# Hidden units of a squared-ReLU MLP kept in DRAM as two parts, one more pair by seven products, and waits of TensorE moved (a two-layer hybrid decoder trunk, fp32)

## The chip, the cores and the metric

The kernel runs on one core of one Trainium2 chip. The metric is the device time of one execution in microseconds; lower is better. Three executions of the kernel before took 2156.13, 2157.28 and 2156.48 us, so the median is 2156.48. A profile was taken of one more execution, of 2157.01 us.

## The reference

Two layers over 256 tokens of width 2048, all in float32. With P the combined projection (1024 columns each of q, k, v, gate_b, gate_c, conv_in):

```python
for l in range(2):
    h = rmsnorm(x, attn_norm_g[l])
    q, k, v, gate_b, gate_c, conv_in = split(h @ w_in[l])        # w_in: 2048 x 6144
    A = diff_attention(qk_norm(q), qk_norm(k), v, lam, rel_bias)  # 8 heads, two maps each
    A = rmsnorm(A, subln_g[l]) * (1 - lam_init)
    C = gate_b * short_conv3(gate_c * conv_in)
    x = x + concat([A, C]) @ w_out[l]                             # 2048 x 2048
    hm = rmsnorm(x, mlp_norm_g[l]) @ w_up[l]                      # 2048 x 8192
    x = x + square(relu(hm)) @ w_down[l]                          # 8192 x 2048
```

The weights are read once per execution; most of the work is the matrix products with them.

## The kernel before

**Products in two parts.** A float32 value is kept as a high part in the type fp32r (a copy by ScalarE, which rounds) and a low part (value minus high part, a subtraction by VectorE). A product is the sum of three matmuls, high by high, high by low, low by high: `TERMS` (line 42). Each weight tile is loaded by a DMA from SyncE's queue, split by ScalarE and VectorE into `hi` and `lo` (class `Weights`, lines 287 to 371) and used by TensorE. `Weights.take` (line 357) hands out the next tile and has the next three (`AHEAD`) made ahead of it.

**The order of the work.** TensorE executes its instructions in the order in which the program issues them. The other engines' instructions are put in an order by a scheduler when the kernel is built, except those that are pinned to program order by `late` (line 122). Small pieces of work that need TensorE (transposes for the norms, attention) are generators kept by `Background` (line 59). After every few matmuls the program calls `work.tick()`, and a piece goes on when its count of ticks has run out; `work.start(piece, wait)` sets the first count. So the number of ticks says where in TensorE's order a transpose lands.

**The mixer** (line 711) runs for two halves of four heads the projections q, k and v and starts `attention` (line 579) behind each as a background piece; the conv path follows, then the output projection `o`. After each 512-column chunk of x is updated, `Norm.chunk` (line 443) is started: it transposes the chunk by TensorE into PSUM banks (`tpn`, from a pool of three), splits the transposed values into the parts `nT` (lines 270 and 271), and sums the squares (`squares`, line 463, on ScalarE).

**The MLP** (line 785) walks the 8192 hidden columns as 32 pairs of 256 (`NP`). In the up stage (line 986 on), pair i gets its two columns by `up_part` (32 matmuls of 128x512 and 32 of 128x256), `evict` adds the two PSUM halves into `h`, and `square` applies ReLU, the ratio of the norms and the square. Two pairs later (`LAG`), the left half of the down projection (output columns 0 to 1023) is formed with pair i's units by the seven products of a Strassen-like scheme (Winograd's form): a 2x2 block product by seven products of blocks (`product`, line 979) in place of eight. It needs sums of blocks of the weights (`quarters`, line 823, with VectorE) and of the units (`S1` to `S4`). Each pair by seven products is 21 matmuls of 128x512; by the ordinary way it is 24 (`ordinary`, line 1052). The last two pairs of the left half are done the ordinary way; before them `seven_onto` (line 1039) adds the seven products to x.

The units are also needed for the right half (columns 1024 to 2047), which comes after the whole up stage. They are therefore written to DRAM from GpSimd's queue: `hid`, one tile per block of four 128-unit groups, 256 KB for an ordinary pair (lines 961 and 962), and `hid7`, 512 KB with the block sums, for the eight pairs of `SEVEN` (line 39), which the right half forms by seven products. In the right half `pair(i)` (line 1083) reads units back into `back`, and ScalarE and VectorE split them into `fb` (lines 1079 and 1080), one pair ahead of TensorE in program order and up to four buffers deep (`apool`). Pairs 24 to 29 are read as blocks 12 to 14 and done column chunk by column chunk (`columns`, line 1105); chunk 2 of the output is one step ahead of chunk 3 (`order`, line 890). At the end of each chunk two instructions `onto` (line 1035) add the accumulators to x, and either the next layer's `norm.chunk` is started or the result is stored.

For the first pair of the up stage, both columns go into one PSUM tile of two banks (line 991), and column 0 is evicted before column 1's last matmuls are issued (lines 996 and 997). The first two forms of its weight tile (`plain`, the splits of single quarters, and `sums`, the block sums and their splits) are made by `forms["begin"]`, called after the square (line 999).

## Time and profile before

| | before |
|---|---|
| median of three executions | 2156.48 us |
| profiled execution | 2157.01 us |
| its span, from the first to the last instruction | 2155.2 us |
| mean granted TensorE clock | 0.999 |
| TensorE busy | 2136.4 us (99%) |
| VectorE busy | 1696.0 us (79%) |
| ScalarE busy | 1335.9 us (62%) |
| GpSimd busy | 160.3 us (7%) |
| DMA traffic | 452.91 MB, mean 210 GB/s |
| of it from GpSimd's queue | 44.17 MB |

One execution was recorded by the hardware profiler, and times in it are counted from the start of the span. In the view of the groups, "out<-in" gives the program's names for the tiles, then partitions x elements and type, and "mean" is the time of one instruction from its start to its end. Matmuls overlap each other, so their mean is longer than the distance from one start to the next. In the view of the waits, "PE pr L1059 <- DVE f L974: 3.0, 2, 1.5" reads: TensorE's instructions of line 1059 on the tile pr waited for VectorE's instruction of line 974 on f, 3.0 us in all, in 2 places, the longest 1.5 us. In the timeline each line is a start, a duration, engine and line, the operation, a count where several of one kind stand together, and in brackets the idle time ahead of it and what ended it. PE is TensorE, PEld its weight load, DVE VectorE, ACT ScalarE, POOL GpSimd, SP SyncE. The work of layer 1 follows that of layer 0 at a distance of about 1073 us: the same wait is found at 164 and at 1237 us.

### The profile page before, as it was taken

How to read it: one execution, taken by the hardware profiler on the slowest of the kernel's cores; microseconds unless marked ns; L12 is line 12 of the kernel's file. 1: busy time of each engine (PE TensorE's matmuls, PEld its weight loads, DVE VectorE, ACT ScalarE, POOL GpSimd, SP SyncE). 2: the span in 40 equal slices, each digit the busy share in tenths (PEclk: the TensorE clock that was granted, in tenths of full speed). 3: DMA queues.
4: the chain of work that ended last, by engine and by line, in shares of the span. 5: the costliest groups of instructions: out<-in, count | busy, mean ns of one | idle time of the engine just before them, and what ended most of it. 6: DMA issues, size and time to landing. Idle time of an engine off the chain costs nothing. (4 is left out here: it accounts for less than half of the span.)

```text
span 2155.2 us, 29063 instructions
## 1 busy us (share of the span) xinstructions
PE 2136.4 (99%) x10940; PEld 1821.8 (85%) x10940; DVE 1696.0 (79%) x2315; ACT 1335.9 (62%) x1799; POOL 160.3 (7%) x228
## 2 busy tenths in 40 slices
PE   9999999999999999999999999999999999999999
PEld 8888888888888888888788888888888888888887
DVE  6777655699889898798666776557998889887985
ACT  6666445567666666566556664445767666675663
POOL 3111100000000000200001111000000000002000
PEclk9999999999999999999999999999999999999999
DMA  8555766577767667686555567655776676766863
GB/s 272 179 160 186 236 187 189 163 237 225 234 214 225 215 220 224 212 296 220 190 166 177 165 203 218 186 175 186 236 232 220 213 227 220 223 209 232 300 225 110
DMA packets 282044, 452.91 MB, mean 210 GB/s; under 512 B 10707, under 2 KB 191525, under 8 KB 281904
## 3 DMA queue, kind: packets, MB, share of 16 engines
q1 hardware_dynamic: 268768, 406.88, 59.6%
q0 software_dynamic: 13088, 44.17, 5.7%
q8 instruction: 85, 1.39, 0.3%
q14 instruction: 55, 0.45, 0.1%
q10 hardware_dynamic: 48, 0.02, 0.0%
HBM read 428.98 MB, written 22.04 MB: 209 GB/s over the span
## 5 line engine op out<-in xcount | busy, mean ns | idle before, releaser
L303 DVE TENSOR_TENSOR wlo<-raw,whi 128x1024 fp32r<-128x1024 f32 x286 | 354.1, 1240 | 237.4 <-ACT whi L302 232.7
L302 ACT ACTIVATE whi<-raw 128x1024 fp32r<-128x1024 f32 x286 | 302.9, 1060 | 321.6 <-PE o L386 73.6
L939 PE MATMUL upc<-nT,uhi 128*128 128x512 f32 x1920 | 477.7, 391 | 0.3 <-ACT ev L949 0.3
L811 ACT ACTIVATE uhi<-uraw 128x1024 fp32r<-128x1024 f32 x256 | 270.2, 1056 | 265.1 <-PE upc L939 235.8
L939 PEld LDWEIGHTS upc<-nT,uhi 128*128 128x128 f32 x1920 | 352.7, 188 | 68.9 <-ACT ev L949 0.7
L812 DVE TENSOR_TENSOR ulo<-uraw,uhi 128x1024 fp32r<-128x1024 f32 x256 | 312.2, 1220 | 83.2 <-ACT uhi L811 78.7
L939 PEld LDWEIGHTS upc<-nT,ulo 128*128 128x128 f32 x1920 | 261.9, 190 | 18.7
L939 PE MATMUL upc<-nT,ulo 128*128 128x256 f32 x1920 | 267.7, 282 | 0.0
L1059 PE MATMUL dn<-whi,fb 128*128 128x512 f32 x512 | 160.3, 389 | 0.0
L386 PE MATMUL o<-whi,cat 128*128 128x512 f32 x512 | 159.5, 390 | 0.0
L302 ACT ACTIVATE whi<-uraw 128x1024 fp32r<-128x1024 f32 x64 | 67.9, 1061 | 78.2 <-PE dn L1059 68.6
L1059 PEld LDWEIGHTS dn<-whi,fb 128*128 128x128 f32 x512 | 96.1, 188 | 20.1
L386 PEld LDWEIGHTS o<-whi,cat 128*128 128x128 f32 x512 | 96.2, 188 | 19.7
L386 PE MATMUL o<-wlo,cat 128*128 128x512 f32 x256 | 99.6, 389 | 0.0
L1059 PE MATMUL dn<-wlo,fb 128*128 128x512 f32 x256 | 99.6, 389 | 0.0
L303 DVE TENSOR_TENSOR wlo<-uraw,whi 128x1024 fp32r<-128x1024 f32 x64 | 78.2, 1221 | 23.4 <-ACT whi L302 23.4
L832 DVE TENSOR_TENSOR t24l<-t,t24h 128x1024 fp32r<-128x1024 f32 x76 | 92.9, 1223 | 3.8 <-ACT t24h L831 1.4
L832 DVE TENSOR_TENSOR t13l<-t,t13h 128x1024 fp32r<-128x1024 f32 x76 | 92.8, 1221 | 3.5 <-ACT t13h L831 2.1
L982 PE MATMUL pr<-t13h,f 128*128 128x512 f32 x240 | 93.8, 391 | 0.0
L832 DVE TENSOR_TENSOR b2l<-draw,b2h 128x1024 fp32r<-128x1024 f32 x76 | 92.4, 1216 | 0.8 <-ACT b2h L831 0.8
L845 DVE TENSOR_TENSOR t<-draw 128x1024 f32<-128x1024 f32 x76 | 92.5, 1217 | 0.0
L831 ACT ACTIVATE t24h<-t 128x1024 fp32r<-128x1024 f32 x76 | 79.9, 1051 | 8.3 <-PE dn L982 3.6
(403 smaller groups left out, 4147.8 us busy)
## 6 DMA issues: line engine op xcount, KB each, us to landing
uraw<-in_w_up_dram SPq DMA_DIRECT2D x128, 1024.0 KB, 6.1
raw<-in_w_in_dram SPq DMA_DIRECT2D x191, 512.0 KB, 4.0
draw<-in_w_down_dram SPq DMA_DIRECT2D x80, 1024.0 KB, 6.9
raw<-in_w_out_dram SPq DMA_DIRECT2D x64, 512.0 KB, 3.7
uraw<-in_w_down_dram SPq DMA_DIRECT2D x32, 1024.0 KB, 6.6
raw<-in_w_down_dram SPq DMA_DIRECT2D x16, 1024.0 KB, 5.0
hid<-h POOLq DMA_DIRECT2D x44, 256.0 KB, 3.7
back<-hid POOLq DMA_DIRECT2D x32, 256.0 KB, 4.2
```

Source lines behind the costliest of these rows:

```text
L302: pair = (nc.scalar.activation(hi, raw, AF.Copy), nc.vector.tensor_sub(lo, raw, hi.bitcast(F32)))
L303: nc.vector.tensor_sub(lo, raw, hi.bitcast(F32)))
L386: nc.tensor.matmul(acc[:, t], a.ap[:, pa, k % KG, t * P:(t + 1) * P], (hi, lo)[pw][:, j], start=(k == 0 and n == 0), stop=(k == nk - 1 and ...
L811: nc.scalar.activation(hi, src, AF.Copy)
L812: nc.vector.tensor_sub(lo, src, hi.bitcast(F32))
L831: keep(nc.scalar.activation(hi, src, AF.Copy))
L832: keep(nc.vector.tensor_sub(lo, src, hi.bitcast(F32)))
L845: keep(nc.vector.tensor_sub(t[:, 0:2], raw[:, :, 1], raw[:, 0]))
L939: nc.tensor.matmul(acc[:, 0] if part else acc, wt[:, k], a.ap[:, 0, k % KG] if part else a.ap[:, :, k % KG], start=(part == 0 and kh == 0 ...
L982: nc.tensor.matmul(prods[n], f[:, pa, a], b[pw], start=(start and m == 0), stop=(stop and m == 2))
L1059: nc.tensor.matmul(prods[p], f[:, pa, 2 * k + t], b[pw][:, n], start=(p in starts and k == 0 and m == 0), stop=(stop and k == 1 and m == 2))
```

## The change

1. `SEVEN` has nine pairs, (2, 4, 7, 9, 12, 14, 17, 19, 22), in place of eight.
2. For an ordinary pair, `hid` holds the two parts of the units, high and low, 512 KB of type fp32r, one tile per pair. They are written from `f` after its split instead of from `h` ahead of it. Reading them back is one DMA (for a block of two pairs, two) into `fb`, and neither ScalarE nor VectorE works on them. Pairs of `SEVEN` are kept, read and split as before.
3. Up stage, first pair: both columns are evicted after all their matmuls; `plain` is called ahead of the evictions and `sums` after the square. The split of the second pair's first weight tile is pinned to program order.
4. `seven_onto` takes no engine; its four adds are on VectorE in both halves, and for the left half they are issued after the two ordinary pairs instead of ahead of them.
5. `Norm.chunk`: the squares are summed at once, ahead of the transposes, except in the first norm of layer 0. At the end of a layer the chunks 0 and 1 of the next norm start after 6 and 11 ticks, not 8 and 16.
6. Attention of the second half of the heads starts after 9 ticks, not 6.
7. In the last layer the last block of chunk 3 is done token tile by token tile (`by_token`): all its matmuls for the first 128 tokens, then those for the other 128.

```diff
-SEVEN = (2, 5, 8, 11, 14, 17, 20, 23)
+SEVEN = (2, 4, 7, 9, 12, 14, 17, 19, 22)
...
             a = self.tiles[n].open()
+            at_once = (self.which, self.l) != (0, 0)
+            if at_once:
+                self.squares(n)
...
             self.tiles[n].ready = True
-            if (self.which, self.l) == (0, 0) and n < D // CH - 1:
+            if at_once:
+                return
+            if n < D // CH - 1:
                 yield 12 - 2 * n
             self.squares(n)
...
                 work.start(attention(l, qT, kT, kL, v, h0, cat[half], bias, tmp,
-                                     1 + half), 3 * (1 + half))
+                                     1 + half), 3 + 6 * half)
...
-                    nc.scalar.activation(hi, src, AF.Copy)
-                    nc.vector.tensor_sub(lo, src, hi.bitcast(F32))
+                    pair = (nc.scalar.activation(hi, src, AF.Copy),
+                            nc.vector.tensor_sub(lo, src, hi.bitcast(F32)))
+                    if (i, c, kh) == (1, 0, 0):
+                        for ins in pair:
+                            late(ins)
...
-                    begin = lambda: made.update(p=plain(), s=sums())
-                    forms["begin"] = begin
+                    forms["plain"] = lambda: made.update(p=plain())
+                    forms["sums"] = lambda: made.update(s=sums())
...
-            hid = [dram.tile([P, KG * S], F32, name=f"hid{l}{b}") for b in range(NB2 - 1)]
+            hid = {i: dram.tile([P, 2, 4 * P], F32R, name=f"hid{l}p{i}")
+                   for i in range(NP - LAG) if i not in SEVEN}
...
                 nc.scalar.activation(u, u, AF.Square)
-                if i not in SEVEN and i < NP - LAG:
-                    nc.gpsimd.dma_start(hid[i // 2][:, i % 2 * 2 * S:(i % 2 + 1) * 2 * S], u)
...
                 nc.vector.tensor_sub(f[:, 1, :n], h[:, :n], f[:, 0, :n].bitcast(F32))
+                if i in hid:
+                    nc.gpsimd.dma_start(hid[i], f[:, :, 0:4].rearrange("p a k c -> p a (k c)"))
                 return f
...
                             up_part(two[c], kh)
-                            if kh:
-                                evict(two[c], h[:, 2 * c:2 * c + 2])
+                    forms["plain"]()
+                    for c in range(2):
+                        evict(two[c], h[:, 2 * c:2 * c + 2])
                     fs[0] = square(0, h)
-                    forms["begin"]()
+                    forms["sums"]()
...
-                for dst, v in ((x11, e1), (x12, e4), (x21, e3), (x22, e3)):
-                    engine.tensor_tensor(dst, dst, v, op=ALU.add)
+
+                def add():
+                    for dst, v in ((x11, e1), (x12, e4), (x21, e3), (x22, e3)):
+                        nc.vector.tensor_add(dst, dst, v)
+
+                return add
...
-            seven_onto(0, nc.gpsimd)
+            add = seven_onto(0)
...
                 ordinary(fs[j], (8,) if j == NP - LAG else (), j == NP - 1)
+            add()
...
-            def read_back(src, pool, tag, n):
...
+            def pair(i, f=None, at=0):
+
+                if f is None:
+                    f = apool.tile([P, 2, 8, P], F32R, tag="a", name="fb")
+                if i not in SEVEN:
+                    nc.gpsimd.dma_start(
+                        f[:, :, at:at + 4].rearrange("p a k c -> p a (k c)"), hid[i])
+                    return f
+                back = fpool.tile([P, 8, P], F32, tag="h", name="back", bufs=1)
+                nc.gpsimd.dma_start(back.rearrange("p a c -> p (a c)"), hid7[i])
+                nc.scalar.activation(f[:, 0], back, AF.Copy)
+                nc.vector.tensor_sub(f[:, 1], back, f[:, 0].bitcast(F32))
+                return f
+
+            def block(b):
+
+                pool, tag = (fpool, "f") if b == BLK else (apool, "a")
                 f = pool.tile([P, 2, 8, P], F32R, tag=tag, name="fb")
+                for j in range(2):
+                    pair(2 * b + j, f, 4 * j)
                 return f
...
+            def by_token(f, n):
+
+                parts = [weights.take() for _ in range(KG // 2)]
+                for t in range(NT):
+                    for k in range(KG):
+                        for m, (pa, pw) in enumerate(TERMS):
+                            nc.tensor.matmul(
+                                accs[n][:, t], f(k, pa, t), parts[k // 2][pw][:, k % 2],
+                                start=False, stop=(k == KG - 1 and m == 2))
+                        work.tick()
...
-            seven_onto(2, nc.vector)
+            seven_onto(2)()
             if not last:
-                work.start(norm.chunk(0, 2), 8)
-                work.start(norm.chunk(1, 2), 16)
+                work.start(norm.chunk(0, 2), 6)
+                work.start(norm.chunk(1, 2), 11)
...
-                columns(lambda k, pa, t, f=blocks[b]: f[:, pa, 2 * k + t], n,
-                        stop=(b == NB2 - 2))
+                units = lambda k, pa, t, f=blocks[b]: f[:, pa, 2 * k + t]
+                if last and (b, n) == order[-1]:
+                    by_token(units, n)
+                else:
+                    columns(units, n, stop=(b == NB2 - 2))
```

More of the change, by code (lines that the diff above doesn't have):

```diff
@@ L1037, in onto, with seven_onto @@
                                                op0=ALU.mult, op1=ALU.add)
-            def seven_onto(n, engine):
+            def seven_onto(n):
                 x11, x21, x12, x22 = (xs[n + i][:, t] for i in range(2) for t in range(NT))
@@ L1071, in mlp @@
                     onto(xs[n][:, t], prods[((2, 4), (3, 8))[n][t]], xs[n][:, t])
-            def read_back(src, pool, tag, n):
-                back = (fpool.tile([P, 8, P], F32, tag="h", name="back", bufs=1) if n == 8 else
-                        nat.tile([P, 4, P], F32, tag="wide", name="back"))
-                nc.gpsimd.dma_start(back.rearrange("p a c -> p (a c)"), src)
+            def pair(i, f=None, at=0):
[12 more added lines that the diff above has]
+                pool, tag = (fpool, "f") if b == BLK else (apool, "a")
                 f = pool.tile([P, 2, 8, P], F32R, tag=tag, name="fb")
-                nc.scalar.activation(f[:, 0, :n], back, AF.Copy)
-                nc.vector.tensor_sub(f[:, 1, :n], back, f[:, 0, :n].bitcast(F32))
-                return f
-            def pair(i):
-                if i in SEVEN:
-                    return read_back(hid7[i], apool, "a", 8)
-                return read_back(hid[i // 2][:, i % 2 * 2 * S:(i % 2 + 1) * 2 * S], apool, "a", 4)
-            def block(b):
-                return read_back(hid[b], *((fpool, "f") if b == BLK else (apool, "a")), 8)
+                for j in range(2):
+                    pair(2 * b + j, f, 4 * j)
+                return f
             def store(n):
```

## The prediction

> **What bounds the kernel now.** The page gives TensorE 2136.4 of 2155.2 us, so I first asked at what pace it issues and where it stands still. The matmul groups' mean of 390 ns is a latency. The pace stands in the windows and the timeline: ninety 128x512 matmuls fill 20 us, and two together last 0.62 where one lasts 0.39, so they start 0.227 apart.
>
> ```profile
> 1980.00:2000.00 20.00, 20.00 (x90) 16.54 (x89) 19.31 (x22) 13.47 (x16) 1.92 (x4) 1.00 1.01 360
> 2000.00:2020.00 20.00, 20.00 (x90) 16.57 (x89) 19.94 (x22) 12.42 (x15) 2.15 (x4) 1.00 0.88 316
> 1069.19 0.62 PE L1112 MATMUL dn<-whi,fb 128*128 128x512 f32 x2
> ```
>
> (The windows' columns: TensorE, its weight loads, VectorE, ScalarE, GpSimd, granted clock, DMA share, GB/s.) The time is therefore the number of matmuls times the pace, plus what TensorE waits. VectorE at 19.94 of 20 us here costs nothing, since all ninety matmuls ran. TensorE's waits, second view:
>
> ```profile
> PE pr L1059 <- DVE f L974: 3.0, 2, 1.5
> PE atp L672 <- DVE mx L605: 3.0, 2, 1.5
> PE tpn L451 <- DVE nT L271: 2.7, 1, 2.7
> PE up L939 <- DVE nT L271: 1.5, 2, 0.7
> PE up L939 <- ACT ev L949: 1.4, 2, 0.7
> PE pr L982 <- DVE t13l L832: 1.2, 2, 0.6
> PE upc L939 <- ACT ev L949: 0.3, 1, 0.3
> ```
>
> That is 13.1 us; each wait also costs 0.1 to 0.25 us of pipeline refill, seen as the excess of the start-to-start distance over the pace. Third, the timeline at these places.
>
> The wait of L1059: a VectorE subtraction of 128x512, 683 ns elsewhere, lasts 3.75 while GpSimd adds x (L1050).
>
> ```profile
> 899.89 3.77 POOL L1050 TENSOR_TENSOR x<-x,e 128x512 f32<-128x512 f32 x3
> 900.48 3.75 DVE L974 TENSOR_TENSOR f<-h,f 128x512 fp32r<-128x512 f32 x1
> 904.28 0.73 PE L1059 MATMUL pr<-whi,f 128*128 128x512 f32 x2 [1.52 <-DVE f L974]
> ```
>
> The layer boundary: transposes wait 2.67 for a bank, and behind them pairs of matmuls last 1.05 instead of 0.62; the granted clock falls.
>
> ```profile
> 1074.92 1.09 PE L451 MATMUL tpn<-ident,x 128*128 128x128 f32 x4 [2.67 <-DVE nT L271]
> 1076.66 1.05 PE L1112 MATMUL dn<-whi,fb 128*128 128x512 f32 x2
> ...
> 1072.00:1076.00 4.00, 1.33 (x8) 1.12 (x7) 2.89 (x5) 1.69 (x5) 1.89 (x2) 0.82 0.00 0
> 1076.00:1080.00 4.00, 4.00 (x15) 3.19 (x14) 0.00 (x0) 0.22 (x1) 0.00 (x0) 0.75 0.00 0
> ```
>
> And the up stage's start, the end, and the hidden units' transfers:
>
> ```profile
> 400.27 0.97 PE L939 MATMUL up<-nT,uhi 128*128 128x512 f32 x3 [0.75 <-DVE nT L271]
> 403.10 1.19 PE L939 MATMUL up<-nT,uhi 128*128 128x512 f32 x4 [0.69 <-ACT ev L949]
> 2150.69 1.41 DVE L1036 SCALAR_TENSOR_TENSOR x<-dn,rowf,x 128x512 f32<-128x512 f32 x2 [5.84 <-PE dn L1112]
> hid<-h POOLq DMA_DIRECT2D x44, 256.0 KB, 3.7
> back<-hid POOLq DMA_DIRECT2D x32, 256.0 KB, 4.2
> ```
>
> **The change, part by part.** The base is the profiled execution, 2157.0 us (span 2155.2 and 1.8 around it); it is 0.5 above the median of 2156.5.
>
> *Nine pairs by seven products.* A pair by products takes 21 matmuls, an ordinary one 24. One more such pair per layer takes away 3 x 2 layers x 0.227 = 1.36 us: **-1.4**.
>
> *Units kept as two parts.* Per layer, ScalarE and VectorE lose the splits of 15 ordinary pairs and 3 blocks (616 and 683 ns per pair); a product pair costs VectorE 7.6 us (five of 128x1024 at 1.15, three of 128x512 at 0.6, start to start), an ordinary one 2.3. VectorE's right half falls from about 107 to 102 of 124 us. None of it is on TensorE's path, so it is worth 0 alone. It costs transfers: each ordinary unit is written and read as 512 KB, not 256. In the right half's 24 pairs 24 MB of weights and 8 MB of units become 24 and 12: 303 GB/s over 124 us, under the 360 that the window above shows. The reads go from GpSimd's queue straight into four buffers, some three pairs (15 us) before use; 512 KB reads land in 3.7 to 5.5 us. That lead hides them. The product pairs' reads stand in the same queue behind an ordinary read that waits for a buffer, still 15 us early. The writes (512 KB, some 7 us) have the 15.9 us of a unit (53 matmuls at 0.227, 32 of 128x256 at 0.120), and now hold f, of which there are two. I take 0; the ends are 0 and the DMA rival below.
>
> *The start of the up stage.* Three waits, with refill 0.92 + 0.85 + 0.77 and 0.11 behind each: 2.87 us a layer. The second arises because column 0's eviction reads the PSUM tile whose other half column 1 needs. Both evictions now follow the matmuls, so nothing is in the way. The first: squares and the second unit's weight split stood ahead of the last nT on ScalarE and VectorE; by the new order they follow. The third: the sums move behind the square, the plain splits before it; by rows t13l ends at about 421.9, and TensorE needs it at 422.9. What is late next is the draw loads: issued near 392.5, they land at 403.4 and 405.8, and ScalarE now asks for them at 404.3 and 405.9, with the eviction and a uhi queued behind; TensorE has 2.7 us of slack there. Gain 2 x 2.87 = **-5.7**; ends: -6.3 (the 0.56 at 466 us, layer 0 only, goes too) and 0.
>
> *The adds of the first left half go to VectorE* and behind the ordinary pairs. The subtraction of L974 is then 0.68 again, done at about 901.8, where TensorE wants it at 902.6: 1.79 x 2 = **-3.6**. VectorE pays four adds of 0.68; the cover is that it no longer splits 15 units. Next late: ScalarE's split of product pair 2 stands ahead of a whi and waits for a read landing at about 907; wlo is then ready at 913.4 where TensorE wants 913.3. I take +0.15 a layer, **+0.3**; ends 0 and +2 (a read 1 us later).
>
> *The boundary.* Squares go first and chunks start at 6 and 11 ticks, not 8 and 16. The last two chunks' transposes then no longer ask for a third bank while VectorE holds it: the second group's sum is ready 1.5 us after the first, 1.2 before TensorE wants it. Gone are 2.8 of waiting and the slow clock: from 1074.92 to 1078.45 four transposes took 0.3 and seven matmuls 1.2 more than at pace: **-4.3**; ends -4.3 and 0. The granted clock was 0.82 and 0.75 in two windows of 4 us, which is half speed for 3.4 us, and 1.00 on both sides: I read it as following from the wait. The Trainium skill, "TensorE: Matmul & The Clock Gate", under "Part 1: The HAM clock gate", says that the clock halves after an idle window of about 3.4 us; its length agrees, but the idle time here was only 2.67. By that threshold the wait would not be the cause and this part would be -2.8, the whole 1.5 us higher.
>
> *Attention's second half starts at 9 ticks, not 6.* The wait of 1.48 on mx has the transposes of the first half behind scores of the second. By the new order they come first; but scores then wait for VectorE's L682 (about 0.75), and transposes and value products later by 0.25 to 1.0 each. I sum 2.5 to 2.9 a layer against 2.05. Ends -1.6 and +1.0 a layer; such small waits are within what my hand sums can miss, so **0**.
>
> *Last block by token tiles.* Both final sums onto x (0.7 each) still wait, in the program, for the last matmul of the accumulator pair. So the 4.6 us of tail stay: **0**, ends 0 and -0.7. Both weight parts are wanted earlier, but VectorE had been idle 5.84 us there.
>
> Sum: -1.4 - 5.7 - 3.6 + 0.3 - 4.3 = -14.7; 2157.0 - 14.7 = 2142.3, or 2141.8 from the median. I say 2142.
>
> **Rivals.**
>
> *Transfers bind (slower).* No transfer of before goes from fp32r to fp32r, so the parts' rate is not shown. If they took twice the engine time per byte, the right half's 36 MB would weigh as 43.5 (45.6e6 bytes); at 353 GB/s that is 129 us for 124, and 6 MB of weights ahead would cover it. At three times it is 151 us, 27 over, of which some 17 are covered: +10 a layer, 2142 + 20 = 2162, slower. It decides from about 9.5 us of starvation per layer. Against it: 256 KB reads land like 512 KB ones, so bytes hardly set it; for it: the share of 1.01 shows the engines full at times. The Trainium skill, "DMA: Bandwidth & Descriptors", under "SWDGE vs HWDGE vs iDMA", says that a transfer into float32r always converts; it gives no rate, and no run here shows one yet.
>
> *The boundary's idle returns elsewhere*, the new chunk order making another transpose wait: 4.3 back, 2146. For it: the layer needs its nT at once whatever the order.
>
> *The up stage's gain is given back*, ScalarE standing at the draw loads: they land up to 12 us at worst where I used 11 to 13, and 2.7 us of slack cover a landing that much later; 2 us beyond it in both layers gives 2146.
>
> *The clock halves for another reason than the wait*: 1.5 us stay, 2143.5. Against it: it fell nowhere else.
>
> *More than forecast*: attention's wait goes and the tail overlaps, -3.2 - 0.7: 2138.
>
> **How the numbers follow.** The forecast 0.60 (alone 2139 to 2146), boundary 0.08, up stage 0.10, clock 0.05, more 0.05, transfers 0.12, of which 0.08 reach slower and 0.03 end within the band. A measurement tells 0.2%, 4.3 us, from no change: faster is under 2152.2, slower over 2160.8. So faster 0.89, same 0.03, slower 0.08; since the cover in attention and the up stage rests on hand sums, I move 0.02 to same. The range 2138 to 2150 leaves out little more than the transfers.
>
> **What would show it.** Right: the waits on f, tpn, up and t13l missing; the granted clock 1.00 at the boundary; 7574 in place of 7580 matmuls of 128x512; one or two waits in attention, no longer on mx; the last sums still starting together behind the last matmul. Wrong: a wait of TensorE on fb ended by a DMA, or DMA share near 1.0 through the right half with fewer than 90 matmuls in 20 us; a wait on uhi near 412 us; more than 3 us a layer in attention.

## The result and the profile after

The changed kernel takes 2152.26 us (median of 14 runs, 2151.12 to 2154.38), the kernel before 2157.30 in the same comparison (14 runs, 2155.57 to 2159.04): the ratio is 0.9978, with a 95% interval of 0.9971 to 0.9985. That is 5.0 us faster where 14.7 were forecast, and just above the range of 2138 to 2150. The profiled execution took 2151.3 us, its span is 2149.5 (2155.2 before).

TensorE's waits in the changed kernel (columns: who waits, for whom, us in all, times, longest):

```profile
PE pr L992 <- DVE f L982: 3.1, 2, 1.7
PE ci L408 <- ACT whi L302: 1.9, 2, 1.6
PE ptp L635 <- DVE s L630: 1.7, 2, 0.8
PE sc L604 <- DVE cat L682: 1.2, 2, 0.6
...
PE av L648 <- DVE pT L638: 1.0, 2, 0.5
PE upc L949 <- ACT ev L959: 0.6, 1, 0.6
```

(Left out is a wait of 1.1 us at the very start, which the kernel before has too.) Set against the list of before: every wait that the change aimed at is gone (f at the ordinary pairs, mx, the bank of tpn, the three at the start of the up stage). But nothing of this list was there before except a shorter wait on ev. The gain was real; a good half of it went into new waits. The signs that the prediction named for being right came, but for one (three waits a layer in attention, not one or two): they looked at the waits that were to go, not at those that could come. With the refill of the pipeline behind each wait, from the start-to-start distances of the two traces:

| place | before, us | after, us | difference | forecast |
|---|---|---|---|---|
| matmuls, six fewer | | | -1.4 | -1.4 |
| start of the up stage | 5.7 | 0 | -5.7 | -5.7 |
| up stage, fourth to sixth unit (ev, f of pair 3) | 0.6 | 4.6 | +4.0 | 0 |
| first left half's end (f), then wlo | 3.6 | 0.7 | -2.9 | -3.3 |
| layer boundary, wait and half clock | 4.3 | 0 | -4.3 | -4.3 |
| attention | 4.1 | 6.0 | +1.9 | 0 |
| conv stage (ci) | 0 | 2.5 | +2.5 | not thought of |
| tail | 4.6 | 4.6 | 0 | 0 |
| sum | | | -5.9 | -14.7 |

The spans differ by 5.7. At the boundary, the windows (columns as in the prediction) now show TensorE busy throughout at full clock:

```profile
1070.00:1074.00 4.00, 4.00 (x22) 3.40 (x20) 1.39 (x2) 1.51 (x3) 1.75 (x2) 1.00 0.00 0
1074.00:1078.00 4.00, 4.00 (x19) 3.30 (x18) 3.54 (x6) 2.90 (x5) 0.15 (x1) 1.00 0.10 18
```

The costliest new wait, that on f of pair 3, here in layer 0 in the timeline of the changed kernel:

```profile
449.22 0.37 SPq L809 DMA_DIRECT2D uraw<-in_w_up_dram  x1
449.82 0.40 SPq L826 DMA_DIRECT2D draw<-in_w_down_dram  x1
...
459.88 0.63 ACT L839 ACTIVATE b1h<-draw 128x512 fp32r<-128x512 f32 x1 [4.14 <-DMA draw<-in_w_down_dram]
...
468.83 1.22 DVE L817 TENSOR_TENSOR ulo<-uraw,uhi 128x1024 fp32r<-128x1024 f32 x1
469.97 1.22 DVE L853 TENSOR_TENSOR t<-draw 128x1024 f32<-128x1024 f32 x1
471.10 1.22 DVE L982 TENSOR_TENSOR f<-h,f 128x1024 fp32r<-128x1024 f32 x1
...
472.38 0.50 PE L992 MATMUL pr<-b1h,f 128*128 128x512 f32 x1 [1.45 <-DVE f L982]
```

The weight tile of pair 4 is issued 0.6 us behind another 1 MB tile and lands 10 us later, at 459.8. ScalarE stands 4.1 us for it, though TensorE wants that tile only at about 488; behind it in ScalarE's order are the square and f of pair 3, whose low part TensorE wants at 470.8. VectorE is then busy without a gap from 460.5 on, and a weight split and a sum stand ahead of f. The same place in the kernel before:

```profile
461.85 0.63 ACT L831 ACTIVATE b1h<-draw 128x512 fp32r<-128x512 f32 x1 [3.70 <-DMA draw<-in_w_down_dram]
...
471.16 1.22 DVE L974 TENSOR_TENSOR f<-h,f 128x1024 fp32r<-128x1024 f32 x1
...
472.54 0.39 PE L982 MATMUL pr<-b1h,f 128*128 128x512 f32 x1
```

There f ended at 472.4, and TensorE came for it at 472.5: it was just covered. The changed kernel brings TensorE there 1.8 us sooner, and f ends at 472.3. The transfer is not all of it: it lands 2.0 us sooner than before (459.8 for 461.8), but f ends 12.5 us behind the landing where it was 10.6, since the scheduler put two more pieces of work (a split and a sum, 1.1 us each from start to start) ahead of it. The time won at the start of the stage was waited out here.

### The profile page after: what moved, and what is told of

It reads as the page before. It is cut to its first block, busy times and chain, and to the rows that moved or that the text cites. A ratio compares the mean times of both kernels' runs of the same rounds, so it can differ in the third digit from the quotient of the medians.

```text
span 2149.5 us, 28983 instructions
## 1 busy us (share of the span) xinstructions
PE 2134.0 (99%) x10934; PEld 1819.9 (85%) x10934; DVE 1678.6 (78%) x2297; ACT 1308.2 (61%) x1767; POOL 169.8 (8%) x226
## 5 line engine op out<-in xcount | busy, mean ns | idle before, releaser
L1074 PE MATMUL dn<-whi,fb 128*128 128x512 f32 x480 | 151.1, 389 | 0.0
L1074 PEld LDWEIGHTS dn<-whi,fb 128*128 128x128 f32 x480 | 90.1, 188 | 18.7
L839 ACT ACTIVATE b2h<-draw 128x1024 fp32r<-128x1024 f32 x78 | 82.5, 1058 | 24.9 <-PE pr L992 22.2
L1074 PE MATMUL dn<-wlo,fb 128*128 128x512 f32 x240 | 93.4, 389 | 0.0
L303 DVE TENSOR_TENSOR wlo<-uraw,whi 128x1024 fp32r<-128x1024 f32 x60 | 73.2, 1224 | 21.1 <-ACT whi L302 20.9
```

Source lines behind the costliest of these rows:

```text
L303: nc.vector.tensor_sub(lo, raw, hi.bitcast(F32)))
L839: keep(nc.scalar.activation(hi, src, AF.Copy))
L1074: nc.tensor.matmul(prods[p], f[:, pa, 2 * k + t], b[pw][:, n], start=(p in starts and k == 0 and m == 0), stop=(stop and k == 1 and m == 2))
```

## The experiments

All are edits of the changed kernel; its 2152.26 is what their medians stand against. The time of each was taken beside runs of the kernel before on the same chip, whose median was 2157.0 to 2157.5 throughout; ratios are to those, with their 95% intervals. The intervals reach 2 to 3 us to each side, so a difference of 1 us between two medians is not clear of noise; where the text leans on one, the trace has to carry it.

### The attention's start back at 6 ticks

```diff
-                                     1 + half), 3 + 6 * half)
+                                     1 + half), 3 * (1 + half))
```

> The changed kernel with the second half's attention started after 6 ticks again, not 9. In the changed kernel's trace TensorE waits 3.0 us a layer inside attention (2.05 before) and 0.6 (layer 0) and 1.9 us (layer 1) on ci for a weight split whose transfer landed behind four prefetched up-stage tiles. Theory A, the tick count caused both: attention goes back to one wait on mx of 1.48 and the waits of ci vanish, 1.9 + 2.5 = 4.4 us less than the changed kernel, about 2148. Theory B, the ci waits come from TensorE arriving earlier or from something else in the change: only 1.9 us less, about 2150.3, and the waits on ci stay.

Measured: 2147.44 us (ratio 0.9956, 0.9941 to 0.9971), 4.8 less. Its waits:

```profile
...
PE atp L677 <- DVE mx L610: 3.0, 2, 1.5
...
PE ci L408 <- ACT whi L302: 0.3, 1, 0.3
```

Theory A: the three extra ticks cost 4.8 us, 1.9 in attention and most of the rest in the conv stage. SyncE's queue shows how. First this kernel, then the changed one (a block in the timeline is a start, a duration, and how many issues):

```profile
1270.47 3.26 SPq L809 DMA_DIRECT2D uraw<-in_w_up_dram  x3
1273.83 4.01 SPq L343 DMA_DIRECT2D raw<-in_w_in_dram  x1
1277.88 1.31 SPq L809 DMA_DIRECT2D uraw<-in_w_up_dram  x1
```

```profile
1273.99 7.39 SPq L809 DMA_DIRECT2D uraw<-in_w_up_dram  x4
1281.48 14.58 SPq L343 DMA_DIRECT2D raw<-in_w_in_dram  x6
```

With 9 ticks four up-stage tiles of 1 MB go out in a row and the conv weights' next load behind them, which lands 10.5 us after its issue at 1292.0; TensorE had wanted it split at 1291.6. With 6 ticks that load takes as long, 10.6 us behind three tiles, but it is issued at 1273.8 and not at 1281.5. How long TensorE waits on ci differs from execution to execution: 1.8 to 4.3 us in all in the thirteen traces with 9 ticks and four buffers, of which the changed kernel's 1.9 is near the low end, and 0 to 0.4 in the three with 6 ticks.

### Only three buffers for those tiles

```diff
-            upool = scope.enter_context(tc.tile_pool(name="upool", bufs=4))
+            upool = scope.enter_context(tc.tile_pool(name="upool", bufs=3))
```

> The changed kernel with three buffers of 1 MB for the up stage's weight tiles instead of four, so that only three of them can be loaded during the conv stage. Theory A, with the later attention start SyncE's queue issues four such loads in a row ahead of the conv weights' next load, and that is why ScalarE's whi is late: the waits on ci (0.6 to 2.5 us a layer in the runs with 9 ticks) fall under 0.5 us. Theory B, the conv weights are late for another reason: they stay above 0.6 us in both layers. The three buffers may cost waits elsewhere in the up stage and the right half, which this run also shows; the time decides nothing.

Measured: no wait on ci is left in its list, at 9 ticks; attention's waits are unchanged (1.7, 1.2 and 1.0 us in all), those of the up stage larger.

```profile
PE pr L992 <- DVE f L982: 3.3, 2, 1.7
PE upc L949 <- ACT ev L959: 1.9, 2, 1.4
...
```

Theory A: the tiles loaded ahead delay the conv weights. The edit changes their place too, not only their number: in layer 1 the three go out from 1257.6 on, 16 us sooner than the four, and no other is issued during the conv stage. The time is 2150.52 (0.9969, 0.9959 to 0.9979), 1.7 less than the changed kernel in spite of the up stage.

### The start of the up stage as before

```diff
-                    forms["plain"]()
-                    for c in range(2):
-                        evict(two[c], h[:, 2 * c:2 * c + 2])
+                            if kh:
+                                evict(two[c], h[:, 2 * c:2 * c + 2])
                     fs[0] = square(0, h)
+                    forms["plain"]()
                     forms["sums"]()
...
-                    if (i, c, kh) == (1, 0, 0):
+                    if False:
```

> The changed kernel with the start of the up stage as before: column 0 evicted before column 1's last matmuls, both forms of the first weight tile made after the square, nothing pinned. Theory A, the up stage's gain is given back at the fifth and sixth units because the engines that feed TensorE are there at the same time as before: the three start waits come back (2.87 a layer) and the waits of 1.7 (layer 0, on f) and 2.9 (layer 1, on ev and f) go or shrink to what they were before, 0.6 in all; the time rises by 5.7 - 4.6 + 0.6 = 1.7 us only, about 2154. Theory B, the new waits come from the parts or the ninth pair: they stay, and the time rises by 5.7, to about 2158.

Measured: 2153.47 (0.9983, 0.9974 to 0.9992), 1.2 more. The waits of the start are back, 1.5, 1.4 and 1.2 in all as before, and those on f of pair 3 and on ev are gone. Theory A: in the trace 5.7 us come back and 4.6 go. The median's 1.2 is close to the sum of 1.7; it is not clear of 0, but it is clear of 5.7.

### Pair 4's tile pinned behind pair 3's units

```diff
-                keep = late if i == 0 or (i == SEVEN[0] and col) else lambda ins: None
+                keep = late if (i in (0, 4) and not col) or (i == SEVEN[0] and col) else lambda ins: None
```

> The changed kernel with the copies, subtractions and sums of the fifth pair's weight tile (left half, pair 4) pinned to program order, that is behind the units of pair 3. In the trace of the changed kernel ScalarE stands 4.1 us at 455.7 to 459.9 for that tile's transfer (10 us, in layer 1 11 us), with the squares, the next weight splits and f of pair 3 queued behind it. Theory A, this standing in the queue is the cause: the waits of TensorE on f and ev at 472, 1533 and 1541 us go, 4.6 us less, about 2147.7. Theory B, VectorE simply has too much to do in this stretch: f stays late or the wait moves to another tile within 20 us, and less than 1.5 us is won.

Measured: 2162.15 (1.0022, 1.0013 to 1.0032), 9.9 more. The waits on f and ev are gone, but TensorE now waits for the pinned tile itself, 3.9 us a layer, and the clock falls behind it:

```profile
PE pr L992 <- DVE t13l L840: 5.5, 2, 2.8
```

Neither theory as stated. Out of ScalarE's way is right, program order is too late: VectorE begins the tile's splits at 489.3 and has the last part that TensorE waits for, t13l, done at 496.6, where TensorE wants the first at about 490.

A second try pinned only the plain quarters, issued earlier (`forms["plain4"]()` behind the first four products of the unit before):

> The changed kernel, but the copies and subtractions of the fifth pair's plain quarters alone are pinned, and issued in program order right after the first four products of the unit before; its sums are left to the scheduler. On ScalarE and VectorE they now stand behind the squares and the parts f of pair 3, so nothing that TensorE wants next waits behind that transfer. Theory A, the order behind a late transfer caused the waits: those on f and ev near 472, 1533 and 1541 us go and none over 0.5 us comes near 490, where pinning everything had made the tile itself late: 3.5 to 4.6 us less than the changed kernel, about 2148.5. Theory B, VectorE has no room in this stretch whatever the order: waits of 1.5 us or more a layer appear on that pair's own parts, and the time stays within 1.5 us of 2152.

Measured: 2149.81 (0.9968, 0.9956 to 0.9980); the waits on f are gone, waits on ev of 1.0 and 0.5 us come at 501 and 1568 us. But so issued, pair 4's tile is loaded ahead of pair 3's, and the sums of pair 4 are formed from pair 3's tile, so this run changes two things and part of the result; it does not settle the cause.

### Without that transfer

```diff
-                    raw = forms["raw"] = load_rows(i, col).rearrange("p k (n c) -> p k n c", n=2)
+                    if (i, col) == (4, 0):
+                        raw = forms["raw"]
+                    else:
+                        raw = load_rows(i, col).rearrange("p k (n c) -> p k n c", n=2)
+                        forms["raw"] = raw
```

> The changed kernel without the left half's load of the fifth pair's weight tile (pair 4): its splits and sums are made from pair 3's tile instead, so one 1 MB transfer a layer is left out and pair 4's part of the left half is computed from the wrong weights. Theory A, ScalarE standing about 4 us for that transfer, with the squares and f of pair 3 queued behind it, makes TensorE wait: the waits on f and ev near 472, 1533 and 1541 us go, 3.5 to 4.6 us less than the changed kernel, about 2148. Theory B, VectorE has no room there whatever arrives when: the wait on f stays with 1 us or more a layer.

Measured: 2150.99 (0.9972, 0.9960 to 0.9984), profiled span 2146.2, 3.3 less than the changed kernel's. Waits on ev: none. That on f is 0.47 us in each layer, where the changed kernel has 1.45 in layer 0 and 1.66 plus 0.65 on ev in layer 1. So Theory A for the larger part, 3.1 of the 4.6 us with refill; 1.5 stay, in which VectorE's order puts a sum and a weight split (1.22 us each) ahead of f. The median is only 1.3 lower, over five executions between 2147.6 and 2153.1, so the reading rests on the trace. The same change of the wait was seen by accident below, where that tile was issued ahead of the other one and landed in 6.1 us.

The other traces show how the two parts of the cause go together. In the changed kernel and in eleven of the runs, those that keep the new start and this tile behind the other one, f of pair 3 ends 12.53 or 12.54 us after the tile has landed, in both layers, with loads that took from 9.2 to 11.9 us: f follows the landing one to one. In the kernel before and with the old start it ends 10.6 us after the landing (once 10.9). So the late load and the 1.9 us of VectorE's new order make the wait together. An estimate from these numbers: with 10.6 in the changed kernel, f would end at 470.4 in layer 0 and 1539.3 in layer 1, where TensorE wants it at 470.8 and 1539.5, and nothing would be waited on f. No run changed that order alone.

### The ninth pair

```diff
-SEVEN = (2, 4, 7, 9, 12, 14, 17, 19, 22)
+SEVEN = (2, 5, 8, 11, 14, 17, 20, 23)
```

> The changed kernel with the old list of eight pairs (2, 5, 8, 11, 14, 17, 20, 23). Theory A, the ninth pair is worth its three matmuls a layer: 6 x 0.227 = 1.4 us more, about 2153.6, and no other wait changes by more than 0.3 us. Theory B, the new spacing by two of product pairs costs waits in the right half that hide part of it: less than 0.7 us more.

Measured: 2153.61 (0.9987, 0.9977 to 0.9996), 1.35 more: Theory A, six matmuls at 0.227 (7580 of 128x512 in its trace, 7574 in the changed kernel's). That the median agrees so closely is in part luck, since the waits on ci alone are 1.1 us longer in its trace (3.0 for 1.9).

### The adds on GpSimd, with parts and without

```diff
-                        nc.vector.tensor_add(dst, dst, v)
+                        (nc.vector if n else nc.gpsimd).tensor_tensor(dst, dst, v, op=ALU.add)
...
-            add = seven_onto(0)
+            seven_onto(0)()
...
-            add()
```

> The changed kernel with the four adds of the first left half on GpSimd and ahead of the ordinary pairs, as before. Theory A, GpSimd's adds slow the VectorE subtraction of L974's kind beside them to about 3.75 us: the wait on f near 900 and 1970 us comes back with 1.5 us and refill, 3.6 us more than the changed kernel, about 2155.8. Theory B, with the splits of the read-back units gone VectorE starts that subtraction earlier, ahead of the adds: no wait, the time within 1 us of the changed kernel.

Measured: 2151.89 (0.9975, 0.9966 to 0.9985), no wait on f near 900 us: GpSimd is back, the wait is not. Theory B has the time right and the reason not: f stands among the adds, not ahead of them. GpSimd's second add first waits 1.03 us for VectorE and runs from 901.40 to 902.70; f begins at 902.56, just before its end, and takes 0.69 us. The third add begins at 902.72. It is two weight splits behind f that are stretched, to 2.3 and 2.2 us, and nobody waits for those. Then the units kept as one part (256 KB, read into a buffer and split), the adds on VectorE as in the change:

```diff
-            hid = {i: dram.tile([P, 2, 4 * P], F32R, name=f"hid{l}p{i}")
+            hid = {i: dram.tile([P, 4 * P], F32, name=f"hid{l}p{i}")
...
+                if i in hid:
+                    nc.gpsimd.dma_start(hid[i], u)
...
-                if i in hid:
-                    nc.gpsimd.dma_start(hid[i], f[:, :, 0:4].rearrange("p a k c -> p a (k c)"))
...
+                    back = nat.tile([P, 4, P], F32, tag="wide", name="back")
+                    nc.gpsimd.dma_start(back.rearrange("p a c -> p (a c)"), hid[i])
+                    nc.scalar.activation(f[:, 0, at:at + 4], back, AF.Copy)
+                    nc.vector.tensor_sub(f[:, 1, at:at + 4], back,
+                                         f[:, 0, at:at + 4].bitcast(F32))
```

> The changed kernel with the ordinary pairs' units kept as one part again: 256 KB written from h, read into a buffer of its own and split by ScalarE and VectorE; the adds of the first left half stay on VectorE behind the ordinary pairs. Theory A, the parts take only work off engines with slack: the time within 1 us of the changed kernel, about 2152, and no wait over 0.5 us near 900 us. Theory B, without the parts VectorE falls behind at the change from the left to the right half: waits of 1 us or more on f or wlo between 895 and 930 us, 3 us or more in all.

Measured: 2153.50 (0.9984, 0.9975 to 0.9994), 1.2 more. Waits that the changed kernel has not, or shorter: 0.9 us on wlo in each layer at 915 and 1988 us, 0.8 on fb in layer 0. Between the theories: the parts are worth 1.2 us by the median, which is not clear of noise, and 2.5 by these waits. Both edits together:

> The same with one part, and the four adds on GpSimd ahead of the ordinary pairs: both halves of the cure for the wait on L974 undone. With parts and GpSimd's adds there was no wait. Theory A, in the kernel before the issues of three reads (1.63 us) stood between GpSimd's first and second add, so that the last three ran in one piece just when VectorE came to f; with one part they stand there again: f takes 3 to 4 us, TensorE waits 1.5 us near 900 and 1970 us, 3.6 us more than the changed kernel, about 2155.8. Theory B, another part of the change moved f: no wait, about 2152.

Measured: 2156.29 (0.9997, 0.9988 to 1.0006), 4.0 more, and the wait is back:

```profile
898.46 1.29 POOL L1063 TENSOR_TENSOR x<-x,e 128x512 f32<-128x512 f32 x1 [24.45 <-ACT e L1055]
899.69 1.63 POOL L1094 DMA_DIRECT2D back<-hid0p  x3
901.34 3.77 POOL L1063 TENSOR_TENSOR x<-x,e 128x512 f32<-128x512 f32 x3
901.93 3.74 DVE L984 TENSOR_TENSOR f<-h,f 128x512 fp32r<-128x512 f32 x1
...
905.72 0.50 PE L1074 MATMUL pr<-whi,f 128*128 128x512 f32 x1 [1.51 <-DVE f L984]
```

Theory A. The issues of the reads stand between GpSimd's first and second add, the last three adds then run in one piece, and f, which comes 0.6 us after they began, ends only 0.6 us after they do. Either half of the change cures it: adds on VectorE, or parts, whose reads go straight into `fb` and are issued at 893.9, ahead of all four adds.

### The boundary's ticks

```diff
-                work.start(norm.chunk(0, 2), 6)
-                work.start(norm.chunk(1, 2), 11)
+                work.start(norm.chunk(0, 2), 8)
+                work.start(norm.chunk(1, 2), 16)
```

> The changed kernel with the next norm's chunks 0 and 1 started after 8 and 16 ticks, as before; the squares stay ahead of the transposes. Theory A, the ticks alone decide: the transposes wait 2.7 us near 1073 us, the granted clock is at half for one window of 3.4 us behind it, and the time is 4.3 us more than the changed kernel, about 2156.5. Theory B, the earlier squares are what freed VectorE and ScalarE: no wait over 0.5 us at the boundary and no change of the time.

Measured: 2156.54 (0.9996, 0.9987 to 1.0006), 4.3 more: Theory A. The agreement to the tenth is luck: the ten executions lie between 2153.3 and 2161.3, and the profiled one, the slowest, has two more windows at half clock, behind waits of 1.87 and 1.83 on ci. The wait of 2.67 is back and the clock with it (windows):

```profile
1072.00:1076.00 4.00, 1.57 (x14) 1.25 (x12) 2.52 (x5) 2.65 (x5) 1.16 (x2) 1.00 0.01 4
1076.00:1080.00 4.00, 3.75 (x14) 3.06 (x15) 0.49 (x2) 0.00 (x0) 0.74 (x1) 0.69 0.00 0
```

The squares' place alone does not take the wait away; whether the new ticks need it was not tried.

### The tail

```diff
+                    for t in range(NT):
+                        onto(xs[2 + n][:, t], accs[n][:, t], xs[2 + n][:, t])
+                    ends = [bank(f"end{t}") for t in range(NT)]
+                    by_token(units, n, ends)
+                    continue
...
-                    columns(units, n, stop=(b == NB2 - 2))
+                    columns(units, n, stop=(b == NB2 - 2 or (last and (b, n) == order[-2])))
...
-                                accs[n][:, t], f(k, pa, t), parts[k // 2][pw][:, k % 2],
-                                start=False, stop=(k == KG - 1 and m == 2))
+                                ends[t], f(k, pa, t), parts[k // 2][pw][:, k % 2],
+                                start=(k == 0 and m == 0), stop=(k == KG - 1 and m == 2))
                         work.tick()
+                    onto(xs[2 + n][:, t], ends[t], xs[2 + n][:, t])
+                    nc.sync.dma_start(
+                        out[0, t * P:(t + 1) * P, (2 + n) * CH:(3 + n) * CH], xs[2 + n][:, t])
```

> The changed kernel with the last block of chunk 3 summed into two banks of its own, one per token tile; the sum so far is added to x while it runs, and each token tile is added and stored as soon as its own matmuls are done. Theory A, the changed kernel's order by token tiles bought nothing only because both additions waited for one accumulator pair: the end then comes 0.7 us sooner, the tail behind the last matmul 3.9 us instead of 4.6. Theory B, the landing of the last store sets the tail whatever stands ahead of it: under 0.3 us.

In the changed kernel the two last additions stand together behind the last matmul, as in the kernel before; here one does:

```profile
2146.78 0.75 DVE L1047 SCALAR_TENSOR_TENSOR x<-end,rowf,x 128x512 f32<-128x512 f32 x1 [1.97 <-PE end L1131]
```

From the last matmul's end to the span's end it is 3.9 us, 4.6 in the changed kernel: Theory A in the trace. The median, 2152.74 (0.9980, 0.9971 to 0.9990), does not show 0.7 us among executions that differ by more.

### The transfers' margin

```diff
+            spare = {i: dram.tile([P, 2, 4 * P], F32R, name=f"spare{l}p{i}") for i in hid}
...
                         f[:, :, at:at + 4].rearrange("p a k c -> p a (k c)"), hid[i])
+                    nc.gpsimd.dma_start(spare[i], hid[i])
                     return f
```

> The changed kernel with every ordinary unit's read followed on GpSimd's queue by a copy of the same 512 KB from DRAM to DRAM: the right half moves 7.5 MB more in 24 pairs, as if the parts took twice the engine time. The outputs do not use the copies. Theory A, the transfers have margin: the DMA share of the right half rises from about 0.85 towards 1.0, TensorE waits nowhere on fb or a weight there, the time within 1 us of the changed kernel. Theory B, they are at their limit: waits of TensorE on whi or fb ended by a late transfer between 920 and 1070 us, 5 us or more in all.

Measured: 2148.25 (0.9962, 0.9948 to 0.9975). It does not answer its question: the scheduler issued the copies in the up stage, right behind the writes, and the right half's rate stayed at 284 GB/s. But the new order happened to put pair 4's tile ahead of the other one (issued at 449.6, the other at 450.7). It landed in 6.1 us, not 10, and the wait on f is 0.47 in both layers, as without the transfer. Then each unit written back from `fb` after it has landed (`nc.gpsimd.dma_start(spare[i], f[...])`):

> The changed kernel with every ordinary unit's parts written back to DRAM from the buffer into which they were read, after they have landed: 512 KB more for each such pair in the right half, with GpSimd's queue standing still until the read has landed. Theory A, the transfers have margin: the right half's rate rises from about 280 to 330 GB/s or more, TensorE waits nowhere there over 0.5 us for whi or fb, and the time is within 1.5 us of the changed kernel. Theory B, they are near their limit: waits on fb or whi of 5 us or more in all between 920 and 1070 us, the time 2157 or more.

Measured: 2149.95 (0.9971, 0.9960 to 0.9981). The right half's windows, first the changed kernel, then with the echo:

```profile
920.00:1060.00 140.00, 140.00 (x623) 116.01 (x622) 113.91 (x115) 79.76 (x91) 17.03 (x25) 1.00 0.86 287
```

```profile
920.00:1060.00 140.00, 140.00 (x623) 116.04 (x622) 113.19 (x115) 80.47 (x92) 29.52 (x43) 1.00 1.05 357
```

70 GB/s more, a DMA share of 1.05, and all 623 matmuls in the same 140 us, without a wait on fb or whi: Theory A. The time is 2.3 us below the changed kernel's, more than the 1.5 that it allowed; in the trace the waits on f of pair 3 are shorter (1.4 and 0.9), the loads having taken 9.9 and 9.4 us.

### What was won, put together

The attention's start at 6 ticks, the last block in its own banks, and in one of two versions also the first half's transposes 2 ticks earlier (`yield 10 if pace == 1`).

> The changed kernel with the second half's attention after 6 ticks as before, the transposes of the first half's result after 10 ticks instead of 12, so that both stand ahead of the second half's first scores, and the last block in banks of its own. Theory A: the wait of 1.48 on mx goes without the later waits growing, the waits on ci stay under 0.5 us, the tail is 0.7 us shorter: the time is that with 6 ticks, 2147.4, less 3.2 and 0.7, about 2143.5. Theory B, the normalised attention output is not ready 2 ticks earlier: the wait moves to it with 1 us or more a layer, and only the tail is won, about 2146.7.

Measured: 2148.76 (0.9959, 0.9946 to 0.9971). The wait on mx became one of 1.91 on cat in each layer, ended by VectorE's split behind the transposes; the later waits did not grow. Theory B in effect, and 2 us above its number; in the trace the clock halved behind one of the two waits. Without that edit:

> The changed kernel with the second half's attention after 6 ticks as before and the last block in banks of its own. The gains should add: 2147.4 with 6 ticks, 0.7 less for the tail, about 2146.7. If the tail is worth nothing the time is that with 6 ticks alone.

Measured: 2146.99 (0.9958, 0.9944 to 0.9972), the lowest median of the study and 5.3 less than the changed kernel. Against 6 ticks alone it is 0.45 less, about what the tail should give, though the runs do not tell these two apart.

## Why the prediction was wrong

The direction was right and the size was not: 5.0 us for 14.7. What was to go went; three terms of the sum failed by what came in its place. The start of the up stage was booked at its full 5.7, and 4.0 of it were waited again at the fourth to sixth unit; attention was taken as 0 and cost 1.9; the conv stage was not in the sum and cost 2.5. That is 8.4 of the 9.0 us by which the spans miss the forecast. By its steps:

- *Nine pairs*: -1.4 forecast, six matmuls fewer, 1.35 by undoing it. Right.
- *Two parts*: 0 forecast, worth 1.2 us by a median that is not clear of noise and 2.5 by waits; the transfers had more margin than the text needed. The fp32r transfers were no slower class: their reads land in 5.9 to 6.4 us beside other loads, and 70 GB/s more on top changed nothing. That rival, the one on the slower side, is refuted for this kernel. The Trainium skill's page "DMA: Bandwidth & Descriptors" says under "SWDGE vs HWDGE vs iDMA" that such a transfer converts; no run here shows a price for that.
- *The start of the up stage*: the step that failed most. All three waits went, as said, and the prediction named the draw loads as what is late next; but it looked only at the first two, and only at the slack of the next unit. It did not ask when the engines behind would be level again. In the kernel before, f of pair 3 had come just in time; it stands behind the tile of pair 4, a 1 MB load that takes 10 to 11 us behind another one, and by the new order two more pieces of VectorE's work stand ahead of it. So TensorE, coming sooner, waited 1.7 and 2.9 us there. Net 1.2 to 1.7, not 5.7. The rival "the gain is given back" had the right substance (ScalarE standing at a draw load), with a price of 4 us and a chance of 0.10 that was too small, and named the wrong unit.
- *The adds*: the wait went, and either of two causes is enough; the prediction credited the move to VectorE. With the parts the move is worth nothing (2151.89 for 2152.26); without them 2.8 us (2153.50 for 2156.29). The wait on wlo came as said, 0.34 a layer for 0.15.
- *The boundary*: -4.3 forecast, 4.3 by undoing it. The clock did follow from the wait: with the wait it halves, without it it does not. The Trainium skill, "TensorE: Matmul & The Clock Gate", "Part 1: The HAM clock gate", has the clock halve after an idle window of about 3.4 us; the length agrees with the 3.41 us at half clock in these traces, and the threshold does not, since the wait was 2.67.
- *Attention*: 0 taken between -1.6 and +1.0 a layer; +1.0 measured. The hand sum of 2.5 to 2.9 against 2.05 already pointed that way; taking 0 was a choice for the convenient value, against the text's own rule for ends far apart.
- *The conv stage*: missing. The text followed the moved attention on TensorE, VectorE and ScalarE, and not on SyncE's queue, where the later end of attention's work regrouped the loads: four tiles in a row for three, and the conv weights' load behind all of them. 2.5 us.
- *The tail*: 0, right, and for the reason given.

Undoing one part at a time gives +1.35, +1.2, +1.2, -0.4 and +4.3 for the five parts that help or do nothing, and -4.8 for the attention's ticks. Only the last two are clear of noise by their medians, and the sum, 2.9, is not the 5.0 measured: the parts and the adds cover for each other, and undone together they give +4.0. What stays open is the 1.5 us of the wait on f that are left without the late transfer. VectorE's order there, a sum and a weight split ahead of f, is read from the timelines; it was not tried by an edit that changes that order alone, nor is it known why the scheduler chose it.

## What to carry to other kernels

A wait taken off the front engine at the start of a stage is a loan until the engines behind it have slack again: follow the feeding chain, loads included, to the first place where the front engine was only just covered, and book the gain less what is waited there. A moved piece of work moves loads too: read the order of the DMA queue before and after, since here a 1 MB load landed after 10.0 us behind another one and after 6.1 ahead of it, and a load of 512 KB went out at 1281.5 us where it had gone out at 1273.8. And where two edits each remove a wait, undo them one at a time and together before crediting one.

## What the runs showed of the hardware

Whether the granted clock fell went by the length of TensorE's idle time, in the traces of all eighteen kernels (the two compared and the sixteen of the experiments; the wait at the very start and the end are left out): of 42 waits between 1.05 and 1.79 us none came with half clock; of four between 1.83 and 1.91 three did; of ten between 2.16 and 2.75 all, each for 3.41 us (once, with 2.56, for 6.83). So a wait growing from 1.7 to 2.2 us costs up to 1.7 us on top, half of 3.41. This may be one reason why executions of one kernel differ by 3 us: of the changed kernel's fourteen, the four with a mean granted clock of 0.999 took 2153.3 to 2154.4, the ten with 1.000 2151.1 to 2153.4. Of these a trace was kept of one alone, so it is not shown.

Three additions of GpSimd in one piece (901.34 to 905.11) held a VectorE subtraction with two operands in SBUF from its start, 0.6 us after theirs, to 0.6 us after their end (3.74 us for 0.69). Where the subtraction began 0.14 us before the end of one addition and the next began 0.02 us after that end, it took 0.69; the two weight splits behind it then took 2.3 and 2.2 us for 1.2, and GpSimd's last two additions 1.7 and 2.3 us for 1.3.
